# Eight more up products ahead of the dense expert stage, and each row of the second gather used one slot later

## The chip, the cores and the metric

The kernel runs on one core of a Trainium2 chip. The metric is device microseconds (us) of one execution, the median of the runs shown. A profiled execution has a span, from its first to its last instruction, and a time of its own, which is a little longer. Engines are named as in the profile: PE (TensorE), PEld (its weight loads), DVE (VectorE), ACT (ScalarE), POOL (GpSimd) and SP (SyncE, which issues most DMAs).

## The reference

One layer of a hybrid block over 512 tokens of width 1024: a trunk (differential attention beside a gated linear recurrence, merged and projected), and behind it a PEER feed-forward layer with 16384 single-neuron experts. Only the second part matters here. Each token picks 8 x 16 = 128 experts:

```python
q = (hb @ w_q).reshape(PEER_BLOCK, PEER_HEADS, 2, PEER_HALF)
sc = jnp.einsum('thcd,hcnd->thcn', q, sub_keys).astype(jnp.float32)
s1, i1 = lax.top_k(sc[:, :, 0], PEER_TOPK)
s2, i2 = lax.top_k(sc[:, :, 1], PEER_TOPK)
...
top_s, pos = lax.top_k(cand_s, PEER_TOPK)
idx = jnp.take_along_axis(cand_i, pos, axis=-1)
g = jax.nn.softmax(top_s, axis=-1)
u = u_tab[idx]
act = jax.nn.gelu(jnp.einsum('thkd,td->thk', u, hb))
wts = (g * act.astype(jnp.float32)).astype(hb.dtype)
v = v_tab[idx]
return jnp.einsum('thk,thkd->td', wts, v)
```

## The kernel before, in words

The 512 tokens are four blocks of 128. Pass `p0` takes block 0 through the trunk, pass `p1` the other three. The expert layer is then done in two ways.

Blocks 0 and 1 gather. `experts` walks 128 slots; in each, an indirect DMA issued by POOL (L855) brings, for each of the 128 tokens of the block, one row of 2048 numbers (the expert's u and v, 1 MB in all) into one of four buffers `uv`. DVE multiplies the u half with the token and sums (the dot, L862), ACT applies gelu and the weight (L867, L868), and DVE adds the weighted v half to `x1` (L845). The add of a slot is issued behind the dot of the next. A slot's gather is tied to a marked instruction elsewhere in the program (`after(s)`, a dependency given by hand), so that the gathers are spread over the other work. The first gather (block 0) runs beside the trunk of `p1`, the second (block 1, the generator `second`, `table=True`) beside the dense stage.

Blocks 2 and 3 (256 tokens, `NT2`) go through all 16384 experts densely, in 128 chunks of 128 experts. For a chunk, the up product is 8 matmuls of 128x128 by 128x256 over the width and a gelu into a tile `y`; DVE multiplies `y` with the weights that the tokens give to these experts (`o`, L1035); the down product is 4 matmuls of 128x128 by 128x512 that accumulate in `acc` over all chunks. An up product comes in two forms, in `up`: for chunks below `AHEAD` plain, with f32 operands (`u`, and `h2r`, the tokens), and for later chunks split, where `chunk` loads `raw`, ACT rounds it to fp32r (L906), DVE takes the rest (L907), and 24 matmuls form three terms. Split products read the tokens from `p1.h2T`, two tiles of the trunk's pool `ap`.

The order of the dense part:

1. `ups_far`: the first `LEAD` = 26 up products (PSUM tiles `pup`), beside the last top-k work of DVE.
2. `picks_t` transposes the picks (PE `pt`). Then come 16 weight groups (`wbuild`, 16 tokens each): DVE, POOL and ACT build one-hot tiles, PE multiplies them (`pw`, L1010), ACT copies into `wst` (L1011), and SP writes it to a DRAM tensor `w_d` (L1012). An up product (tiles `st`) is given to each group until `AHEAD - 6` are made; the last six are written behind the groups.
3. SP loads the weights back (`w`, L1023), the last two groups' part behind the last write, and the 128 downs follow; from the 24th on, one more (split) up product goes with each down until all are made.

The instructions of an engine run in the order in which a scheduler, working from a simulated timeline, has put them; it may move an up product ahead of where the code has it. `share` counts fractions of a slot (0.2 for each of the far products, 0.5 a weight group, 0.6 a down, 1.1 a down with an up) and starts the next slot of the second gather when a whole one is owed.

## Time and profile before

| | |
|---|---|
| runs | 1903.67 us median of 3 (1903.01 to 1905.06) |
| profiled execution | 1902.58 us, span 1900.8 us |
| PE busy | 1742.3 us (92%) |
| PEld busy | 1371.8 us (72%) |
| DVE busy | 1309.5 us (69%) |
| ACT, POOL busy | 781.8 us (41%), 483.3 us (25%) |
| moved by DMA | 563.37 MB, mean 296 GB/s |
| mean granted clock of PE | 0.949 |

The up products of the dense stage start 933.8 us into the span, the first down at 1193.97. A busy share is a mean over stages with different limits; the rows below are cut by stage for that reason. PE's clock is given as a share of its full 2.4 GHz; 0.5 is its lower level, 1.2 GHz. Matmuls are pipelined; an f32 matmul shows as two records, an fp32r matmul as one.

### The profile page before, as it was taken

The page shows a single profiled execution, that of the slowest core. Times are in us where ns is not written, and L with a number is a line of the kernel's source. Part 1 is how long each engine was busy: PE and PEld are TensorE (multiplying, and loading weights), DVE is VectorE, ACT ScalarE, POOL GpSimd, SP SyncE. Part 2 cuts the span into 40 slices and gives each one's busy share as a digit, 9 for nine tenths or more (in the row PEclk, how much of TensorE's full clock was granted, in tenths as well). Part 3 has the DMA queues.
Part 4 walks back from the last instruction along what each step waited for, and adds up shares of the span by engine and source line. Part 5 has one row for each costly group of instructions (what it writes and reads, how often), then busy time and mean ns, then how long its engine had stood idle before and what let it go on. Part 6 is the DMA issues. An engine that isn't in the chain of part 4 may idle for free.

```text
span 1900.8 us, 25745 instructions
## 1 busy us (share of the span) xinstructions
PE 1742.3 (92%) x9166; PEld 1371.8 (72%) x9166; DVE 1309.5 (69%) x2818; ACT 781.8 (41%) x2193; POOL 483.3 (25%) x375
## 2 busy tenths in 40 slices
PE   7899898889959899979996984899999999999998
PEld 6689797778849677769985884346776677667763
DVE  2241387989999987689999467446676667666662
ACT  3382333767768744254412565012322232222210
POOL 1100001535332233242001365222222232222220
PEclk9899897889969899999998998899999999999999
DMA  7478554887888899987464578999999999999893
GB/s 297 144 272 315 181 186 158 308 291 269 328 287 298 322 400 356 369 310 255 153 220 144 183 274 310 356 373 393 370 367 389 378 365 369 348 350 363 328 354 122
DMA packets 131471, 563.37 MB, mean 296 GB/s; under 512 B 11408, under 2 KB 43280, under 8 KB 88592
## 3 DMA queue, kind: packets, MB, share of 16 engines
q1 hardware_dynamic: 94480, 293.29, 42.6%
q0 software_dynamic: 36864, 268.45, 37.3%
q8 instruction: 72, 1.18, 0.2%
q14 instruction: 55, 0.45, 0.1%
HBM read 539.68 MB, written 22.02 MB: 296 GB/s over the span
## 4 chain that ended last, share of the span: by engine, by line
PE 60%; DVE 14%; issue 9%; DMA 8%; ACT 5%; POOL 3%; DVEq 0%; SPq 0%; POOLq 0%; ACTq 0%
PE acc L210 22%; PE st L210 16%; DMA uv<-in_uv_dram,idx 6%; PE ppq L210 5%; PE pkq L210 5%; POOL uv L855 3%; DVE x1f L845 2%; DVE uv L862 2%; PE pw L1010 1%; PE pvv L210 1%; DMA v<-in_v_t_dram 1%; PE pgt L210 1%; PE psc L511 1%; DVE wl L231 1%; PE pbR L687 1%
## 5 line engine op out<-in xcount | busy, mean ns | idle before, releaser
L855 POOL DMA_INDIRECT uv<-in_uv_dram,idx x256 | 360.0, 1406 | 1067.6 <-DVE x1g L845 265.7
L210 PE MATMUL acc<-v,o 128*128 128x512 f32 x1024 | 449.9, 595 | 20.8 <-DVE o L1035 18.6
L210 PEld LDWEIGHTS acc<-v,o 128*128 128x128 f32 x1024 | 191.8, 191 | 244.9 <-issue 222.4
L210 PE MATMUL st<-a,t 128*128 128x256 f32 x2136 | 282.2, 292 | 0.0
L210 PEld LDWEIGHTS st<-a,t 128*128 128x128 f32 x2136 | 262.5, 191 | 22.5 <-issue 19.6
L845 DVE SCALAR_TENSOR_TENSOR x1g<-uv,e,x1g 128x1024 f32<-128x1024 f32 x128 | 164.1, 1282 | 47.6 <-ACT e L868 47.6
L845 DVE SCALAR_TENSOR_TENSOR x1f<-uv,e,x1f 128x1024 f32<-128x1024 f32 x128 | 163.8, 1280 | 17.2 <-ACT e L877 17.0
L862 DVE SCALAR_TENSOR_TENSOR uv<-uv,h2f 128x1024 f32<-128x1024 f32 x128 | 155.6, 1218 | 28.9 <-DMA uv<-in_uv_dram,idx 28.5
L862 DVE SCALAR_TENSOR_TENSOR uv<-uv,h2g 128x1024 f32<-128x1024 f32 x128 | 155.9, 1218 | 19.6 <-DMA uv<-in_uv_dram,idx 19.6
L867 ACT ACTIVATE e<-e 128x1 f32<-128x1 f32 x128 | 25.9, 202 | 341.4 <-DVE uv L862 341.0
L907 DVE TENSOR_TENSOR t<-raw,t 128x1024 fp32r<-128x1024 f32 x89 | 108.8, 1223 | 74.5 <-ACT t L906 74.5
L1035 DVE TENSOR_TENSOR o<-y,w 128x256 f32<-128x256 f32 x104 | 44.0, 423 | 99.8 <-PE acc L210 99.7
L924 ACT ACTIVATE y<-st 128x256 f32<-128x256 f32 x89 | 34.1, 383 | 179.7 <-PE st L210 177.5
L231 DVE TENSOR_TENSOR wl<-raw,wh 128x1024 fp32r<-128x1024 f32 x76 | 90.9, 1217 | 23.8 <-PE pgt L210 9.5
L906 ACT CAST t<-raw 128x1024 fp32r<-128x1024 f32 x89 | 92.0, 1034 | 25.1 <-PE acc L210 25.1
L210 PE MATMUL pup<-r,u 128*128 128x256 f32 x416 | 90.6, 379 | 1.0 <-DMA u<-in_u_t_dram 1.0
L230 ACT CAST wh<-raw 128x1024 fp32r<-128x1024 f32 x76 | 76.7, 1043 | 28.2 <-PE pwo L714 10.4
L210 PEld LDWEIGHTS pup<-r,u 128*128 128x128 f32 x416 | 78.7, 190 | 12.3 <-issue 1.7
L1010 PE MATMUL pw<-o1s,o 128*128 128x128 f32 x512 | 68.8, 289 | 17.7 <-DVE o L994 13.3
L1009 POOL TENSOR_SCALAR o1s<-iota,r 128x128 f32<-128x128 bf16 x64 | 70.8, 1114 | 41.7 <-issue 14.8
L1010 PEld LDWEIGHTS pw<-o1s,o 128*128 128x128 f32 x512 | 64.5, 199 | 22.8 <-ACT wst L1011 5.7
L210 PE MATMUL pkq<-wh,a 128*128 128x256 f32 x384 | 77.8, 297 | 0.0
(266 smaller groups left out, 3235.5 us busy)
## 6 DMA issues: line engine op xcount, KB each, us to landing
v<-in_v_t_dram SPq DMA_DIRECT2D x64, 1024.0 KB
raw<-in_u_t_dram SPq DMA_DIRECT2D x89, 512.0 KB
u<-in_u_t_dram SPq DMA_DIRECT2D x39, 512.0 KB
w<-in_w_br_dram SPq DMA_DIRECT2D x16, 1024.0 KB
w_d<-wst SPq DMA_DIRECT2D x16, 1024.0 KB
w<-w_d SPq DMA_DIRECT2D x9, 1536.0 KB
w<-in_w_qkv_dram SPq DMA_DIRECT2D x12, 1024.0 KB
raw<-in_w_qkv_dram SPq DMA_DIRECT2D x24, 512.0 KB
```

The source lines that it names most:

```text
L210: nc.tensor.matmul(o, lhs[a], rhs[b], start=start and i == 0, stop=stop and i == len(terms) - 1)
L230: A.copy(hi[:, i : i + 1024], raw)
L231: V.tensor_tensor(lo[:, i : i + 1024], raw, hi[:, i : i + 1024].bitcast(F32), op=ALU.subtract)
L845: V.scalar_tensor_tensor(x1, v_, e_, x1, op0=ALU.mult, op1=ALU.add)
L855: i = nc.gpsimd.indirect_dma_start(out=t, out_offset=None, in_=uv, in_offset=bass.IndirectOffsetOnAxis(ap=idx[:, s : s + 1], axis=0),)
L862: i = V.scalar_tensor_tensor(t[:, 0:D], t[:, 0:D], 1.0, h2, op0=ALU.mult, op1=ALU.mult, accum_out=d)
L906: A.copy(t[:, 0, :], raw)
L907: V.tensor_tensor(t[:, 1, :], raw, t[:, 0, :].bitcast(F32), op=ALU.subtract)
L924: return A.activation(o, S_, AF.Gelu_apprx_tanh)
L1009: e.tensor_scalar(o1, iota, k1, g1, op0=ALU.is_equal, op1=ALU.mult)
L1010: nc.tensor.matmul(pw[:, j, :], o2[:, j, :], o1, start=True, stop=True)
L1035: turn[0] = V.tensor_mul(o.rearrange("p (g t) -> p g t", g=NG), yv, ws[c // WI][:, :, c % WI, :])
```

## The change

It has two parts. In the dense stage `AHEAD` goes from 39 to 47 (`SPARE` = 8 more plain up products, kept in a tile `spare`), `LEAD` from 26 to 31, and the last six (`HELD`) may not be scheduled before the last matmul of the last weight group. Split up products then go with the downs from the 32nd on, so that 81 instead of 89 are split. Their tokens are no longer read from `p1.h2T` but from `h2s`, two tiles that ACT and DVE form from `h2r`; the pool `ap` closes with the trunk to make room, and the trunk's pools stay open until the keys are done. In the second gather (`late`), the dot of a slot, the add of the slot before and the two ACT operations are written behind the issue of the next slot's gather, and the dot may not be scheduled before that slot's marked instruction.

```diff
--- before.py
+++ after.py
@@ -90,9 +90,9 @@
     pp = ctx.enter_context(tc.tile_pool(name="pp", bufs=2))
     dram = ctx.enter_context(tc.tile_pool(name="dram", bufs=1, space=bass.MemoryType.DRAM))
     wp = ctx.enter_context(tc.tile_pool(name="wp", bufs=4))
-    ap = ctx.enter_context(tc.tile_pool(name="ap", bufs=1))
     rg = ctx.enter_context(tc.tile_pool(name="rg", bufs=5))
     trunk = ctx.enter_context(ExitStack())
+    ap = trunk.enter_context(tc.tile_pool(name="ap", bufs=1, side="right"))
     s4 = trunk.enter_context(tc.tile_pool(name="s4", bufs=2, side="right"))
     s2 = trunk.enter_context(tc.tile_pool(name="s2", bufs=5, side="right"))
 
@@ -206,10 +206,13 @@
 
     def mm(o, lhs, rhs, start, stop):
         terms = [(0, 0)] if len(lhs) == 1 or len(rhs) == 1 else [(0, 0), (0, 1), (1, 0)]
-        for i, (a, b) in enumerate(terms):
+        made = [
             nc.tensor.matmul(
                 o, lhs[a], rhs[b], start=start and i == 0, stop=stop and i == len(terms) - 1
             )
+            for i, (a, b) in enumerate(terms)
+        ]
+        return made[0]
 
 
     in_turn = mybir.DependencyInfo(mybir.DependencyClass.Sync, mybir.DependencyReason.SCHED_ONLY)
@@ -849,24 +852,38 @@
             if not table and s < SLOTS:
                 tc.add_manual_dep(i.ins, after(s).ins.name, in_turn, reason="in turn")
 
+        def late(s, t, d, q, w):
+
+            i = V.scalar_tensor_tensor(t[:, 0:D], t[:, 0:D], 1.0, h2, op0=ALU.mult, op1=ALU.mult, accum_out=d)
+            if s + 1 < SLOTS:
+                tc.add_manual_dep(i.ins, mark.ins.name, in_turn, reason="in turn")
+            if before:
+                add(*before.pop(0))
+            A.activation(q, d, AF.Gelu_apprx_tanh)
+            A.activation(w, q, AF.Copy, scale=picks[1][:, s : s + 1])
+            before.append((t[:, D : 2 * D], w))
+
+        waiting = None
         for s in range(SLOTS):
             idx, g = picks
+            mark = after(s)
             t = uvp.tile([P, 2 * D], F32, tag="uv", name=nm("uv"))
             i = nc.gpsimd.indirect_dma_start(
                 out=t, out_offset=None, in_=uv,
                 in_offset=bass.IndirectOffsetOnAxis(ap=idx[:, s : s + 1], axis=0),
             )
-            tc.add_manual_dep(i.ins, after(s).ins.name, in_turn, reason="in turn")
+            tc.add_manual_dep(i.ins, mark.ins.name, in_turn, reason="in turn")
             e = sm.tile([P, 3], F32, tag="e", name=nm("e"))
             d, q, w = e[:, 0:1], e[:, 1:2], e[:, 2:3]
-            i = V.scalar_tensor_tensor(t[:, 0:D], t[:, 0:D], 1.0, h2, op0=ALU.mult, op1=ALU.mult, accum_out=d)
-            behind(i, s + 1)
-            if before:
-                add(*before.pop(0))
             if table:
-                A.activation(q, d, AF.Gelu_apprx_tanh)
-                A.activation(w, q, AF.Copy, scale=g[:, s : s + 1])
+                if waiting:
+                    late(*waiting)
+                waiting = s, t, d, q, w
             else:
+                i = V.scalar_tensor_tensor(t[:, 0:D], t[:, 0:D], 1.0, h2, op0=ALU.mult, op1=ALU.mult, accum_out=d)
+                behind(i, s + 1)
+                if before:
+                    add(*before.pop(0))
 
                 i = A.activation(q, d, AF.Square, scale=GELU_R)
                 behind(i, s + 2)
@@ -875,8 +892,10 @@
                 i = A.activation(w, d, AF.Copy, scale=g[:, s : s + 1])
                 behind(i, s + 2)
                 A.activation(w, q, AF.Identity, scale=w, bias=w)
-            before.append((t[:, D : 2 * D], w))
+                before.append((t[:, D : 2 * D], w))
             yield
+        if waiting:
+            late(*waiting)
         for v_, e_ in before:
             add(v_, e_)
         nc.sync.dma_start(out[t0 : t0 + P, :], x1)
@@ -887,12 +906,13 @@
     NG = NT2 // TG
     NCH = SLOTS
 
-    HEAD, MID = 24, 15
-    AHEAD = HEAD + MID
+
+    HEAD, MID, SPARE = 24, 15, 8
+    AHEAD = HEAD + MID + SPARE
 
     TURN = list(range(HEAD, AHEAD)) + list(range(HEAD)) + list(range(AHEAD, SLOTS))
 
-    LEAD = 26
+    LEAD, HELD = 31, 6
 
     WI = 12
 
@@ -908,17 +928,19 @@
         return t[:, 0, :], t[:, 1, :]
 
 
-    def up(c, S_):
+    def up(c, S_, after=None):
         ks = lambda k: slice(k * P, (k + 1) * P)
         if c < AHEAD:
             u = wp.tile([P, D], F32, tag="raw", name=nm("u"), bufs=3)
             nc.sync.dma_start(u, u_t[c])
             for k in range(KT):
-                mm(S_, [u[:, ks(k)]], [p1.h2r[:, k, :]], k == 0, k == KT - 1)
+                i = mm(S_, [u[:, ks(k)]], [p1.h2r[:, k, :]], k == 0, k == KT - 1)
+                if after is not None and k == 0:
+                    tc.add_manual_dep(i.ins, after.ins.name, in_turn, reason="in turn")
         else:
             uhi, ulo = chunk(u_t, c, "near")
             for k in range(KT):
-                mm(S_, [uhi[:, ks(k)], ulo[:, ks(k)]], [h[:, k, P : 3 * P] for h in p1.h2T], k == 0, k == KT - 1)
+                mm(S_, [uhi[:, ks(k)], ulo[:, ks(k)]], [h[:, k, :] for h in h2s], k == 0, k == KT - 1)
 
     def gelu(o, S_):
         return A.activation(o, S_, AF.Gelu_apprx_tanh)
@@ -951,6 +973,8 @@
 
 
     def kept(c):
+        if HEAD + MID <= c < AHEAD:
+            return spare[:, c - HEAD - MID, :]
         if c >= HEAD:
             return mid.tile([P, NT2], F32, tag="ym", name=nm("y"), bufs=MID)
         if c % WI == 0:
@@ -975,10 +999,10 @@
         pt_ = pool("pt", 2, space=PSUM)
         acc = pa.tile([P, 2, D], F32, tag="acc", name="acc")
 
-        def up_near():
+        def up_near(after=None):
             c = TURN[len(ys)]
             st = pt_.tile([P, 512], F32, tag="st", name=nm("st"))
-            up(c, st[:, 0:NT2])
+            up(c, st[:, 0:NT2], after)
             y = kept(c)
             gelu(y, st[:, 0:NT2])
             ys[c] = y
@@ -1007,9 +1031,10 @@
                     else:
                         e = nc.gpsimd if O1[j] == "P" else V
                         e.tensor_scalar(o1, iota, k1, g1, op0=ALU.is_equal, op1=ALU.mult)
-                    nc.tensor.matmul(pw[:, j, :], o2[:, j, :], o1, start=True, stop=True)
+                    last = nc.tensor.matmul(pw[:, j, :], o2[:, j, :], o1, start=True, stop=True)
                 turn[0] = A.copy(st[:, :, t4 : t4 + 4], pw.rearrange("p t i -> p i t"))
             nc.sync.dma_start(w_d[tg], st)
+            return last
 
         ws, vs = [], []
 
@@ -1040,9 +1065,9 @@
                     mm(acc[:, b, hs], [o[:, bs]], [v_[:, hs]], c == 0, c == NCH - 1)
 
         for tg in range(NG):
-            wbuild(tg)
+            last = wbuild(tg)
             share("w")
-            if len(ys) < AHEAD - 6:
+            if len(ys) < AHEAD - HELD:
                 up_near()
 
             if tg == 7:
@@ -1052,12 +1077,17 @@
                 wload(0, 8, 14)
         wload(0, 14, NG)
         while len(ys) < AHEAD:
-            up_near()
+            up_near(last)
+
+        A.copy(h2s[0], p1.h2r)
+        V.tensor_tensor(h2s[1], p1.h2r, h2s[0].bitcast(F32), op=ALU.subtract)
         for c in range(NCH):
             down(c, ys[c])
-            if c >= HEAD and len(ys) < NCH:
+
+            more = c >= HEAD + SPARE and len(ys) < NCH
+            if more:
                 up_near()
-            share("both" if c >= HEAD and len(ys) < NCH else "down")
+            share("both" if more else "down")
         for b in range(2):
             ob = wp.tile([P, D], F32, tag="raw", name=nm("ob"), bufs=3)
             nc.sync.dma_start(ob, x1_d[1 + b])
@@ -1079,9 +1109,9 @@
     run(p1.rest)
     p1.merge()
     p1.project()
+    run(p1.keys())
     trunk.close()
     mid = ctx.enter_context(tc.tile_pool(name="mid", bufs=1, reuse_waits="tile", side="right"))
-    run(p1.keys())
     when = []
     for name, mark in marks:
         owed[0] += PACE[name]
@@ -1100,6 +1130,9 @@
         yield from experts(P, x1, h2, (p1.idx[:, 0, :], p1.g[:, 0, :]), lambda s: turn[0], True)
 
     ex = second()
+
+    h2s = [mid.tile([P, KT, NT2], F32R, tag=f"h{i}", name=f"h2s{i}") for i in range(2)]
+    spare = mid.tile([P, SPARE, NT2], F32, tag="spare", name="spare")
     ys = ups_far(0, LEAD)
     p1.weights()
     kTs = picks_t()
```

Three places show how the order of the instructions moves. First PE between the last weight group (`pw`) and the first downs (`acc`). Before:

```order
L1010 MATMUL pw_10368<-o1s_10338,o_2093_10369 128x128 x4
L1010 MATMUL pw_10382<-o1s_10338,o_2096_10383 128x128 x4
L210 MATMUL acc<-v_10479,o_10481 128x512 x4
L210 MATMUL acc<-v_10479,o_10487 128x512 x4
L210 MATMUL acc<-v_10500,o_10502 128x512 x4
```

With the change:

```order
L1034 MATMUL pw_10485<-o1s_10441,o_2114_10486 128x128 x4
L210 MATMUL st_10508<-r_6202,u_10509 128x256 x8
L210 MATMUL st_10520<-r_6202,u_10521 128x256 x8
L210 MATMUL st_10532<-r_6202,u_10533 128x256 x8
L210 MATMUL st_10544<-r_6202,u_10545 128x256 x8
L210 MATMUL st_10556<-r_6202,u_10557 128x256 x8
L210 MATMUL acc<-v_10584,o_10586 128x512 x3
L210 MATMUL st_10568<-r_6202,u_10569 128x256 x8
L210 MATMUL acc<-v_10584,o_10586 128x512
L210 MATMUL acc<-v_10584,o_10592 128x512 x4
```

Five whole up products now stand between the two, and a sixth inside the first down. Second, the queue of SP around the last write of the weights (`w_d<-wst`). Before:

```order
L1012 DMA w_d<-wst_10280 128x2048
L1031 DMA v_10479<-in_v_t_dram 128x2x1024
L1031 DMA v_10500<-in_v_t_dram 128x2x1024
L1031 DMA v_10521<-in_v_t_dram 128x2x1024
L1012 DMA w_d<-wst_10339 128x2048
L1023 DMA w_9901<-w_d 128x2x192
L1023 DMA w_10477<-w_d 128x16x192
```

With the change:

```order
L1036 DMA w_d<-wst_10383 128x2048
L1056 DMA v_10584<-in_v_t_dram 128x2x1024
L1056 DMA v_10605<-in_v_t_dram 128x2x1024
L1036 DMA w_d<-wst_10442 128x2048
L1056 DMA v_10626<-in_v_t_dram 128x2x1024
L935 DMA u_10545<-in_u_t_dram 128x1024
L935 DMA u_10557<-in_u_t_dram 128x1024
L1048 DMA w_9980<-w_d 128x2x192
L935 DMA u_10569<-in_u_t_dram 128x1024
L1048 DMA w_10582<-w_d 128x16x192
```

The third load of `v` moves behind the last write, and the loads for the fourth and fifth of the six stand between it and the load of the weights' last part (128x2x192); the sixth one's stands behind that. Third, PE from the last far products (`pup`) through the transposes (`pt`) into the first weight groups. Before:

```order
L210 MATMUL pup_9261<-r_6202,u_9262 128x256 x8
L932 MATMUL pt_1842_9286<-ident,r_6281 128x128 x3
L932 MATMUL pt_1843_9295<-ident,r_6281 128x128 x3
L1010 MATMUL pw_9318<-o1s_9316,o_1847_9319 128x128 x4
L1010 MATMUL pw_9332<-o1s_9316,o_1850_9333 128x128 x4
L210 MATMUL st_9375<-r_6202,u_9376 128x256 x7
L1010 MATMUL pw_9346<-o1s_9316,o_1853_9347 128x128 x4
```

With the change:

```order
L210 MATMUL pup_9328<-r_6202,u_9329 128x256 x8
L954 MATMUL pt_1854_9353<-ident,r_6276 128x128 x3
L954 MATMUL pt_1855_9362<-ident,r_6276 128x128 x3
L210 MATMUL st_9442<-r_6202,u_9443 128x256 x8
L210 MATMUL st_9520<-r_6202,u_9521 128x256 x4
L1034 MATMUL pw_9385<-o1s_9383,o_1859_9386 128x128 x4
L1034 MATMUL pw_9399<-o1s_9383,o_1862_9400 128x128 x4
L210 MATMUL st_9520<-r_6202,u_9521 128x256 x4
L210 MATMUL st_9591<-r_6202,u_9592 128x256 x5
```

Twelve up matmuls now stand ahead of the first weight matmul. Behind them the two kinds alternate, 8 matmuls of `pw` (half a group) and 9 of `st`, eight times (the last with 5); the remaining 192 matmuls of `pw`, twelve groups, stand without up products, where before it was 160, ten groups.

## Rows read from the trace of the kernel before

**Rows 1.** Busy time by stage: PE, PEld, DVE, ACT, POOL, then clock, DMA share, GB/s

```profile
1046.00:1116.00 70.00, 69.57 (x404) 63.89 (x405) 33.63 (x79) 36.70 (x98) 27.38 (x30) 0.96 0.60 209
1116.00:1176.00 60.00, 43.06 (x318) 38.86 (x317) 52.93 (x123) 46.40 (x121) 46.34 (x38) 0.97 0.76 288
1176.00:1194.00 18.00, 0.03 (x1) 0.03 (x1) 2.56 (x5) 0.50 (x2) 1.48 (x1) 0.57 0.80 291
1194.00:1303.00 109.00, 106.84 (x330) 55.03 (x331) 55.56 (x81) 13.98 (x40) 26.78 (x19) 0.98 1.02 385
1303.00:1839.00 536.00, 536.00 (x2703) 371.57 (x2702) 360.12 (x455) 153.53 (x358) 134.74 (x95) 1.00 0.95 364
1839.00:1901.00 62.00, 55.23 (x131) 24.26 (x129) 18.68 (x28) 2.76 (x11) 2.61 (x2) 0.98 0.45 172
```

**Rows 2.** Chain that ended last, pieces of the late stage: start, length, what

```profile
1302.69 6.87 PE acc L210 x16
...
1344.51 5.75 PE st L210 x48
1350.26 6.87 PE acc L210 x16
```

**Rows 3.** The timeline around the first down: PE, then SP's queue

```profile
1173.32 2.02 PE L1010 MATMUL pw<-o1s,o 128*128 128x128 f32 x16 [0.67 <-ACT wst L1011]
1193.97 57.63 PE L210 MATMUL acc<-v,o 128*128 128x512 f32 x128 [18.63 <-DVE o L1035]
1176.36 0.46 SPq L1012 DMA_DIRECT2D w_d<-wst  x1
1190.72 0.88 SPq L1023 DMA_DIRECT2D w<-w_d  x2
```

**Rows 4.** Timeline of PE, end of the far products to the first weight group

```profile
1015.65 10.60 PE L210 MATMUL pup<-r,u 128*128 128x256 f32 x48 [0.95 <-DMA u<-in_u_t_dram]
1044.07 0.90 PE L932 MATMUL pt<-ident,r 128*128 128x128 f32 x3 [5.26 <-DVE r L321]
1046.43 3.78 PE L1010 MATMUL pw<-o1s,o 128*128 128x128 f32 x16 [1.46 <-ACT kTb L937]
```

**Rows 5.** Instructions of the tile pup: count, ns min/median/max, first and last start

```profile
L210 PE MATMUL pup<-r,u x416: 379/379/454, 933.9 to 1025.9; 128*128 128x256 f32 x139
```

**Rows 6.** Timeline of DVE where the second block's picks become ready

```profile
1034.69 1.22 DVE L862 SCALAR_TENSOR_TENSOR uv<-uv,h2g 128x1024 f32<-128x1024 f32 x1
1037.69 1.27 DVE L845 SCALAR_TENSOR_TENSOR x1g<-uv,e,x1g 128x1024 f32<-128x1024 f32 x1
1040.02 2.13 DVE L1009 TENSOR_SCALAR o1s<-iota,r 128x128 f32<-128x128 bf16 x8
1042.79 1.22 DVE L321 TENSOR_REDUCE r<-oh 128x64 f32<-128x1024 bf16 x1
```

**Rows 7.** Timeline of the weight groups: PE with and without ups, one DVE wait

```profile
1106.48 4.05 PE L210 MATMUL st<-r,u 128*128 128x256 f32 x18
1112.15 3.62 PE L210 MATMUL st<-r,u 128*128 128x256 f32 x16
1142.77 1.23 DVE L862 SCALAR_TENSOR_TENSOR uv<-uv,h2g 128x1024 f32<-128x1024 f32 x1 [5.13 <-DMA uv<-in_uv_dram,idx]
1144.75 4.46 PE L1010 MATMUL pw<-o1s,o 128*128 128x128 f32 x24 [5.55 <-DVE o L994]
```

**Rows 8.** Groups of ACT from 1116 to 1176 us: busy us, mean ns | idle before

```profile
L1011 ACT COPY wst<-pw 128x512 f32<-128x512 f32 x40 | 23.1, 578 | 8.1 <-PE pw L1010 8.1
L1006 ACT ACTIVATE o1s<-osq,r 128x128 f32<-128x128 f32 x36 | 16.2, 496 | 0.3 <-DMA w_d<-wst 0.3
L1005 ACT ACTIVATE osq<-iota,r 128x128 f32<-128x128 bf16 x34 | 12.3, 402 | 0.0
```

**Rows 9.** Timeline of the end

```profile
1894.27 2.35 DVE L1064 TENSOR_TENSOR ob<-ob,acc 128x1024 f32<-128x1024 f32 x2 [9.88 <-PE acc L210]
```

**Rows 10.** Waits from 1300 to 1840 us: us in total, times, longest

```profile
POOL uv L855 <- DVE x1g L845: 250.6, 64, 8.9
```

## The prediction

> **What bounds the kernel now.** I read the busy times by stage first. From 1303 to 1839 us PE is busy for all of 536 us at a granted clock of 1.00, its full level, and from 1194 to 1303 for 106.84 of 109 [rows 1]. So from the first down to the end a product is worth its own length, and a wait of DVE, ACT or POOL is not. Ahead of that the same view shows where PE is not full: 43 of 60 us from 1116 to 1176, and nothing in the 18 us before the first down, with the clock at 0.57 at the end of it. The chain of waits gives the late stage's prices: 16 records, two downs, take 6.87 us, so a down 3.433; 48 records, one split product and a second whose down comes later, take 5.75, so a split product 2.875 [rows 2]. The timeline around the first down shows what ended the hole: SP writes the last weights at 1176.36, issues their load at 1190.72, and the first down begins at 1193.97 after 18.63 us of idle PE [rows 3]. A second hole of 18.4 us lies between the end of the far products, 1015.65 + 10.60 = 1026.25, and the first weight matmul at 1046.43; what ends it is DVE, which makes the second block's picks [rows 4].
>
> These prices give the run before back: 1193.97 + 128 downs x 3.433 (439.4) + 89 split products x 2.875 (255.9) = 1889.3. From the first down to 1302.69, where the page's piece begins, 26 downs and 5 split products should take 103.6 us and took 108.7, a loss of 5.1 while PE starts up. With it the sum is 1894.4; the last DVE group, which PE's last down released, begins at 1894.27 [rows 9].
>
> **A, far products.** 26 of them ran from 933.9 [rows 5] to 1026.25 [rows 4], 3.55 us each, stops between them included. Nothing ahead of them moves. 31 end at 933.9 + 31 x 3.55 = 1044.0, so five stand in the hole at no cost. The cover must be there: the picks were ready at 1042.79 + 1.22 = 1044.0 [rows 6]. DVE now makes h2s's second tile ahead of that, twice a 1024-wide f32 pass of 1.22 us (+2.4), and the changed order puts behind it a dot and an add (1.22 + 1.27 [rows 6]) and the eight o1s (2.13). That gives 1041.8. If none of the moves helped it would be 1046.4; that end costs 2.4 us. ACT's cast for h2s is four times a 512-wide copy of 0.578 [rows 8], 2.3 us, in front of gelus that PE does not wait for while its buffers last; I cost it at nothing, at worst 2.3.
>
> **B, four weight groups with products.** From 1044.0: two transposes of 0.9 [rows 4], then 12 up matmuls, 24 records at 3.55/16 = 0.222 (5.3), to 1051.1. Half a group with 9 up matmuls between repeats every 1112.15 - 1106.48 = 5.67 us [rows 7]. Seven such and a last shorter one of 3.9 are 43.6: 1094.7.
>
> **C, twelve groups without.** The ten such groups took from 1112.15 + 3.62 [rows 7] to 1173.32 + 2.02 [rows 3], 59.6 us, 5.96 each. One stop in it was not the groups' own: a dot on DVE waited 5.13 us for its gather and PE 5.55 behind it [rows 7]; without it a group is 5.4. ACT's own three kinds of work come to 51.6 us in it [rows 8], 5.2 a group, so ACT is nearly the bound there, and two groups more cost that too. In `late` a dot stands behind the next slot's mark, so its row has had a slot's time to come, and I expect this stop to go, though a dot can now wait on ACT's copy, which is the mark. I take 5.6, with the ends 5.4 and 5.96: 67.2, and the groups' end T = 1161.9 (1159.5 to 1166.2). It was 1175.3.
>
> **D, the hole before the first down.** It now holds five products; the sixth lies in the first down. The floor stays the path over DRAM, 18.63 us from T, since the write and the load are the same. Three products have their loads at hand: 10.65 us. The fourth and fifth loads can only be issued when the first and second product have freed a buffer, and then stand behind what the queues hold: 18 us x 291 GB/s = 5.2 MB moved in that hole before, with the third v tile (1.05 MB) now in it too. 6.3 MB at 385 GB/s, the best rate of a stage [rows 1], is 16.3 us; no row shows how the queues share, so I let the fourth load land at about 15 and the fifth product end at 22. The ends are 18.6 (the loads slip through) and 25 (they go last). The first down starts at 1161.9 + 22 = 1183.9, 10.1 us earlier than before. The split products' loads, which also stood ahead of the first down before, now come behind; 31 downs cover them.
>
> **E, from the first down to the end.** 439.4 + 81 x 2.875 (232.9) + the sixth product, 3.55 + the loss at the start, 5.1 (none to 5.1, as the hole is now nearly filled) = 681.0, and 1864.9 for the last down. The end after it is unchanged: 1900.8 - 1894.27 = 6.5, a span of 1871.4. The profiled execution before took 1902.58, 1.8 more than its span: 1873.1. Its runs' median stands 1.1 above that time, so **1874**. In parts: 8 split products fewer, -23.0; the first down earlier, -10.1; the sixth product, +3.55.
>
> What `late` itself brings here is little: PE waits for no dot from 1303 to 1839 [rows 1]. It is worth its share of C only. Eight split products fewer also take ACT's roundings and DVE's subtractions away; neither was late, so I count nothing.
>
> **Rivals.** *The transfers take part of it back.* The downs' weights, the split products' loads and the gathers moved 109 x 385 + 536 x 364 = 237 MB by 1839 [rows 1]. Eight loads of 0.52 MB fewer leave 233, and by my sum there are 625.6 us for them, 372 GB/s. The DMA share is already 0.95 there. If 364 were all that the queues give, the stretch would take 640 us, 14 more, and the time be 1888. For it: share 0.95 to 1.02. Against it: 385 GB/s over 109 us, and PE not waiting once in 536 us, so 364 is rather what was asked for. 0.16.
>
> The Trainium skill (DMA: Bandwidth & Descriptors, Specifications) gives a limit of about 358 GB/s from HBM for one core. By that the 233 MB would need 651 us, 25 more, some 1899 (an estimate from that page's figure). Here 385 over 109 us and 364 over 536 stand above it [rows 1], so as a hard limit it does not hold for this core alone; as part of the rival above it gets 0.03 of the chance.
>
> *The gathers run out of buffers (slower).* There are four `uv` buffers, and `late` holds each until the next slot's add. A split product and its down take 6.31 us and owe 1.1 slots: a slot every 5.73 us, four in 22.9. If the buffer came free one slot later, four slots would take 28.7, a slot every 7.16 and so a pair of products 7.88 instead of 6.31. PE would be held through masks that stand behind the waiting dot on DVE: 81 pairs x 1.57 = 127, some 2000 us. For it: POOL already waited 250.6 us, 64 times, for the add that frees a buffer [rows 10]. Against it: in the printed order of DVE a dot stands 2.8 masks behind its mark in this stage, 2.6 before; the add goes with it, so a buffer is held hardly longer. It decides if adds come later against the marks by more than the 8.9 us of the longest wait. 0.03.
>
> That the change does not do what it says can be set aside: the order of PE shows the products where the text says they are.
>
> **How the numbers follow.** Forecast 0.76, the transfers 0.19 with the skill's limit, the buffers 0.03, 0.02 for a stop that I do not see, of which 0.01 ends within 0.2% of before. A measurement of this kernel can tell about 0.2%, 4 us, from no change. Low end: C at 5.4 (-2.4), D at its floor of 18.6 (-3.4), no loss at the start (-5.1) make 1863, and a microsecond for clocks: 1862. High end: C at 5.96 (+4.3), D at 25 (+3), the picks late (+2.4) make 1884; I go on to 1892 to take in the transfers at 364. The forecast's cases and the transfers all end below 1900: faster 0.96, same 0.01, slower 0.03.
>
> **What would show it.** In the timeline of PE: the far products to about 1044 and a weight matmul at about 1051 with no hole of more than 3 us; no up products in the last twelve groups, which end at about 1162; three products at once behind them, a stop of some 4 us, two more, and the first down at about 1184. The w load still about 14 us behind the write. From there no idle PE and 3.433 and 2.875 for a down and a split product. It is wrong if PE shows idle time released by a `v` or `raw` load (the first rival) or by `o` behind a dot (the second), or if the first down stands at 1190 or later, in which case the held loads or the twelve groups were mis-sized, and the timeline tells which.

## The result, and the profile after

| | before | with the change |
|---|---|---|
| median of the runs | 1903.34 us (4, 1900.74 to 1905.06) | 1872.52 us (4, 1867.72 to 1874.02) |
| profiled execution, span | 1900.8 us | 1870.4 us |
| PE busy, mean granted clock | 92%, 0.949 | 93%, 0.956 |

The ratio is 0.9831, with an interval of 0.9811 to 0.9852: faster by 1.7%, 1.5 us under the forecast of 1874. The terms of the sum were less exact than that; some errors were of opposite sign.

Busy time of the changed kernel by stage (stretch, length, then PE, PEld, DVE, ACT, POOL busy with their instructions, PE's clock, DMA share, GB/s), cut at its own events: far products, groups with products, groups without, hole, downs alone, downs with split products, end. It answers to [rows 1].

```profile
934.00:1039.00 105.00, 104.69 (x490) 91.86 (x489) 104.63 (x530) 22.05 (x49) 6.83 (x6) 1.00 0.64 201
1039.00:1088.60 49.60, 49.60 (x296) 45.42 (x295) 29.20 (x68) 28.94 (x83) 24.20 (x22) 1.00 0.64 217
1088.60:1158.60 70.00, 51.21 (x386) 47.06 (x386) 64.88 (x148) 56.42 (x146) 66.25 (x50) 0.98 0.78 285
1158.60:1185.30 26.70, 19.55 (x82) 16.52 (x81) 6.10 (x9) 3.12 (x9) 2.83 (x2) 0.87 1.03 398
1185.30:1298.00 112.70, 108.33 (x258) 49.01 (x256) 49.30 (x75) 9.27 (x33) 24.02 (x18) 0.98 0.98 374
1298.00:1808.00 510.00, 510.00 (x2597) 352.83 (x2596) 344.39 (x437) 147.08 (x342) 136.83 (x90) 1.00 0.95 363
1808.00:1870.00 62.00, 55.80 (x136) 24.83 (x134) 26.73 (x39) 4.25 (x17) 6.97 (x5) 0.97 0.60 226
```

The hole behind the far products is gone, the one before the first down is three quarters full, and PE still never stops once split products go with the downs. In the downs alone PE is idle for 4.4 us, all of it in stops for `v` loads. The kernel before has one such stop there, of 2.16 us:

```profile
1253.76 24.27 PE L210 MATMUL acc<-v,o 128*128 128x512 f32 x56 [2.16 <-DMA v<-in_v_t_dram]
```

PE's timeline of the changed kernel shows where its stops are (start, length, what, records, idle time before it and what ended it); it answers to [rows 3] and [rows 4].

```profile
1009.79 29.52 PE L210 MATMUL pup<-r,u 128*128 128x256 f32 x136
1039.15 0.82 PE L954 MATMUL pt<-ident,r 128*128 128x128 f32 x6
1039.80 5.34 PE L210 MATMUL st<-r,u 128*128 128x256 f32 x24
1044.98 1.95 PE L1034 MATMUL pw<-o1s,o 128*128 128x128 f32 x16
...
1086.47 2.32 PE L210 MATMUL st<-r,u 128*128 128x256 f32 x10
...
1154.95 3.66 PE L1034 MATMUL pw<-o1s,o 128*128 128x128 f32 x30 [3.07 <-POOL o1s L1033]
1158.45 10.53 PE L210 MATMUL st<-r,u 128*128 128x256 f32 x48
1176.13 9.32 PE L210 MATMUL st<-r,u 128*128 128x256 f32 x32 [7.15 <-DMA u<-in_u_t_dram]
1185.29 2.74 PE L210 MATMUL acc<-v,o 128*128 128x512 f32 x6
...
1245.34 41.44 PE L210 MATMUL acc<-v,o 128*128 128x512 f32 x96 [1.50 <-DMA v<-in_v_t_dram]
1289.65 8.80 PE L210 MATMUL acc<-v,o 128*128 128x512 f32 x16 [2.87 <-DMA v<-in_v_t_dram]
```

SP's queue and the chain that ended last show what PE waited for: the fourth held load is issued at 1162.10, behind a write and `v` tiles, and needs 13.89 us; two `v` loads need 21 and 22 us.

```profile
1152.69 6.37 SPq L1056 DMA_DIRECT2D v<-in_v_t_dram  x2
1159.26 0.34 SPq L1036 DMA_DIRECT2D w_d<-wst  x1
1160.99 0.37 SPq L1056 DMA_DIRECT2D v<-in_v_t_dram  x1
1162.10 3.79 SPq L935 DMA_DIRECT2D u<-in_u_t_dram  x2
1172.26 0.38 SPq L1048 DMA_DIRECT2D w<-w_d  x1
```

```profile
1162.10 13.89 DMA u<-in_u_t_dram
...
1224.27 20.93 DMA v<-in_v_t_dram
1245.20 0.14 issue
1245.34 21.81 PE acc L210 x51
1267.15 22.37 DMA v<-in_v_t_dram
```

POOL's wait for the add, which answers to [rows 10], is what it was, and the end [rows 9] starts 6.6 us before the span's end as before:

```profile
POOL uv L871 <- DVE x1g L848: 251.1, 65, 7.6
```

```profile
1863.83 2.35 DVE L1094 TENSOR_TENSOR ob<-ob,acc 128x1024 f32<-128x1024 f32 x2 [9.88 <-PE acc L210]
```

### The profile page after: what moved, and what is told of

It reads as the page before. It is cut to its first block, busy times and chain, and to the rows that moved or that the text cites. A ratio compares the mean times of both kernels' runs of the same rounds, so it can differ in the third digit from the quotient of the medians.

```text
span 1870.4 us, 25606 instructions
## 1 busy us (share of the span) xinstructions
PE 1739.8 (93%) x9102; PEld 1366.9 (73%) x9102; DVE 1303.3 (70%) x2811; ACT 780.0 (42%) x2188; POOL 498.4 (27%) x375
## 4 chain that ended last, share of the span: by engine, by line
PE 73%; DMA 10%; DVE 8%; ACT 4%; issue 4%; POOL 2%; DVEq 0%; SPq 0%; POOLq 0%; ACTq 0%
PE acc L210 22%; PE st L210 15%; PE pup L210 5%; PE ppq L210 5%; DMA uv<-in_uv_dram,idx 5%; PE pgt L210 4%; PE pkq L210 4%; PE pbR L690 4%; PE pbA L683 3%; PE pwo L717 3%; DMA v<-in_v_t_dram 2%; DVE x1f L848 2%; PE pvv L210 2%; PE pw L1034 1%; DVE uv L883 1%
## 5 line engine op out<-in xcount | busy, mean ns | idle before, releaser
L210 PE MATMUL st<-h2s,t 128*128 128x256 f32 x1944 | 252.6, 288 | 0.0
L210 PEld LDWEIGHTS st<-h2s,t 128*128 128x128 f32 x1944 | 235.0, 188 | 20.1 <-issue 17.2
L927 DVE TENSOR_TENSOR t<-raw,t 128x1024 fp32r<-128x1024 f32 x81 | 99.0, 1222 | 69.3 <-ACT t L926 69.3
L210 PE MATMUL pup<-r,u 128*128 128x256 f32 x496 | 107.6, 379 | 0.3 <-DMA u<-in_u_t_dram 0.3
L210 PEld LDWEIGHTS pup<-r,u 128*128 128x128 f32 x496 | 93.9, 190 | 13.4 <-issue 0.8
L926 ACT CAST t<-raw 128x1024 fp32r<-128x1024 f32 x81 | 83.8, 1034 | 23.4 <-PE acc L210 23.4
L1034 PE MATMUL pw<-o1s,o 128*128 128x128 f32 x512 | 66.8, 285 | 18.8 <-ACT wst L1035 8.9
L1033 POOL TENSOR_SCALAR o1s<-iota,r 128x128 f32<-128x128 bf16 x64 | 80.5, 1266 | 10.0 <-issue 4.2
L201 POOL TENSOR_SCALAR sm<-sm 128x1 f32<-128x1 f32 (+4 forms) x24 | 9.6, 398 | 253.6 <-ACT hh L403 111.5
```

The source lines that it names most:

```text
L210: nc.tensor.matmul(o, lhs[a], rhs[b], start=start and i == 0, stop=stop and i == len(terms) - 1)
L926: A.copy(t[:, 0, :], raw)
L927: V.tensor_tensor(t[:, 1, :], raw, t[:, 0, :].bitcast(F32), op=ALU.subtract)
L1033: e.tensor_scalar(o1, iota, k1, g1, op0=ALU.is_equal, op1=ALU.mult)
L1034: last = nc.tensor.matmul(pw[:, j, :], o2[:, j, :], o1, start=True, stop=True)
```

## The experiments

The far products start between 928.3 and 934.3 us in all the profiled executions, of kernels of both sorts (before 933.9, e4 931.0, the change 930.6, e5 932.8). The stage lengths below are therefore taken from an event of the same execution. Runs e1 to e4, e5 to e8, e9 with e10 and e11 with e12 each share a chip and their runs of the kernel before, so their medians can be compared; otherwise the ratios to the kernel before are.

### First group: the two parts, and one piece

**The change again (e1).** 

> The change once more, unaltered, as the yardstick of the runs beside it. If the 3.3 us by which its far products started earlier than in the kernel before (930.63 against 933.93) were only this one execution, they will start between 930 and 934 here, unrelated to the rest; if the change brings them forward, at 930.6 again. Ratio to the kernel before 0.983 to 0.985; the hole between the last weight matmul and the first down is 26 to 27 us again if the held loads' 13.9 us is a property of the order, and nearer 22 if it was an accident of that execution.

Median 1873.29 us, ratio 0.9842 [0.9823, 0.9861]. The far products started at 930.0, the hole was 27.4 us long, the stops for v 2.13 and 1.94 us. Hole and stops belong to the order; the start, with the spread above, does not belong to the change.

**Without the second part (e2).**

```diff
+            i = V.scalar_tensor_tensor(t[:, 0:D], t[:, 0:D], 1.0, h2, op0=ALU.mult, op1=ALU.mult, accum_out=d)
+            behind(i, s + 1)
+            if before:
+                add(*before.pop(0))
             if table:
-                if waiting:
-                    late(*waiting)
-                waiting = s, t, d, q, w
+                A.activation(q, d, AF.Gelu_apprx_tanh)
+                A.activation(w, q, AF.Copy, scale=g[:, s : s + 1])
```

> The change without its second part: the dot of a slot stands again right behind the issue of its own gather, all else as in the change. My theory (the gain is the eight products and the holes, the second part brings little): within 3 us of the change, the twelve groups without products 2 to 4 us longer, since a dot on DVE can wait for its gather in them again, and nothing different behind the first down. Rival (using the rows a slot later is what lets 1.1 slots go by for every pair of products): 10 us or more slower than the change, with PE waiting for o behind a dot.

Median 1878.13 us, ratio 0.9872 [0.985, 0.9894], 4.8 us above the change beside it. The twelve groups took 69.1 us (the change 69.8 and 68.8), so the difference is not there. The same kernel once more:

> The kernel of e2 once more, for a second look at its stops. Theory (they belong to the order): two stops for v at some 60 and 110 us behind the first down again, over 6 us in sum, and 43 us for the 96 records behind the first. Rival (an accident of that execution): 3 to 5 us in sum, as in the change.

Ratio 0.9848 [0.9822, 0.9874], from two runs. The stops in e2 and then in this run (e12):

```profile
1246.75 43.13 PE L210 MATMUL acc<-v,o 128*128 128x512 f32 x96 [4.04 <-DMA v<-in_v_t_dram]
1293.40 8.80 PE L210 MATMUL acc<-v,o 128*128 128x512 f32 x16 [3.52 <-DMA v<-in_v_t_dram]
```

```profile
1038.61 0.52 PE L938 MATMUL pt<-ident,r 128*128 128x128 f32 x3 [1.38 <-DVE r L324]
1041.85 0.87 PE L938 MATMUL pt<-ident,r 128*128 128x128 f32 x3 [2.72 <-DVE r L324]
1042.51 7.39 PE L210 MATMUL st<-r,u 128*128 128x256 f32 x24
...
1249.17 41.44 PE L210 MATMUL acc<-v,o 128*128 128x512 f32 x96 [2.67 <-DMA v<-in_v_t_dram]
1294.18 7.11 PE L210 MATMUL acc<-v,o 128*128 128x512 f32 x16 [3.58 <-DVE uv L865]
```

So the stops were not the same twice: 7.6 us in sum, then 6.3 (expected over 6), and the 43 us behind the first did not come again. The trace names DVE's dot (`uv`) as the end of e12's second stop; the `v` load issued at 1272.00 took 22.0 us and landed at the same time, so the two cannot be told apart there.

What did repeat is in front: PE waits for DVE's picks `r`. Without the second part, five dots and adds of the gather stand ahead of the picks on DVE instead of four (2.5 us a pair), and DVE waits 1.6 us for ACT. The wait and the end of the picks in e12, then the end of the picks in the change:

```profile
1031.53 0.29 DVE L340 TENSOR_REDUCE sm<-r 128x8 f32<-128x128 f32 x1 [1.59 <-ACT r L337]
1040.48 1.22 DVE L324 TENSOR_REDUCE r<-oh 128x64 f32<-128x1024 bf16 x1
```

```profile
1037.57 1.22 DVE L324 TENSOR_REDUCE r<-oh 128x64 f32<-128x1024 bf16 x1
```

Counted from the first far product, the picks are ready at 111.8 us (e2), 113.0 (e12) and 112.9 (e11, below) without the second part and at 108.2 in the change; the first weight matmul comes at 117.5 (e2), 121.1 (e12) and 120.2 (e11), with the second part and the eight products at 113.9 to 115.1 (seven profiles). Not all of this reaches the end. In e12 the first down is 4.5 us later than in the change and the rest takes 0.4 us more; in e2 it is 1.1 us later, and 5.1 us are lost behind it, in the stops and the slower downs behind them. By the ratios the part is worth 1 to 6 us, with intervals that overlap. My theory, which put it into the groups, falls, and so does its rival.

**The second part alone (e3).** The functions `experts` and `late` of the change in the kernel before.

> The kernel before with the second part alone: 39 products ahead as before, the tokens of the split products read from the trunk's tiles as before. My theory: 0 to 6 us faster than the kernel before, all of it in the ten groups without products (59.6 us before, 54 to 58 here); the stretch behind the first down unchanged to 2 us. Rival (it holds buffers longer): slower, with POOL's wait for x1g above 300 us from the first down on (250.6 before). Rival (it carries the gain): faster by over 15 us.

Ratio 1.0007 [0.9993, 1.0021], median 1904.59 us: no difference. The ten groups took 58.6 us instead of 59.6. POOL's wait for x1g from 1300 to 1800 us is 253.3 (before in the same stretch 229.3), and PE never waits for it there. (Earlier, at 1252, the trace puts a stop of PE of 3.6 us down to x1g; a `v` load issued at 1231.45 landed at the same time, after 20.7 us.) Alone, the second part is worth nothing that can be measured. The picks come 109.8 us behind the first far product, in the kernel before 110.1: here the eight o1s still stand ahead of them on DVE, as before.

**The tokens alone (e4; with the wide layout below, e8).** h2s, formed and read as in the change, with `SPARE` 0 and the last six not held.

> The kernel before with one piece of the change: the split products read their tokens from the two compact tiles h2s, not from the trunk's tiles, whose pool closes early; 39 products ahead and the dots as before, the last six products where the kernel before has them. In the trace of the change two split products and two downs came every 12.52 us, in the kernel before every 12.62. Theory (the tiles that the split products read make the difference): 12.52 here too, and 89 x 0.048 = 4.3 us off the time behind the first down; two DVE passes ahead of the picks cost 0 to 2.4 us before it; in sum 2 to 4 us faster than before. Rival (it belongs to the order or to the one execution): 12.62, and 0 to 2.4 us slower than before.

The period was 12.52 us, and the time the same: ratio 1.0001 [0.9986, 1.0016]. The matmuls of the split products, before and here (count, then ns of one, shortest, median, longest):

```profile
L210 PEld LDWEIGHTS st<-a,t x2136: 187/192/192, 1277.4 to 1838.9; 128*128 128x128 f32 x195
L210 PE MATMUL st<-a,t x2136: 278/283/682, 1277.5 to 1839.0; 128*128 128x256 f32 x195
```

```profile
L210 PEld LDWEIGHTS st<-h2s,t x2136: 186/188/190, 1275.0 to 1836.8; 128*128 128x128 f32 x195
L210 PE MATMUL st<-h2s,t x2136: 277/279/683, 1275.0 to 1836.9; 128*128 128x256 f32 x195
```

Each is 4 ns shorter. But the first weight matmul came 116.1 us behind the first far product (before 112.5): ahead of the picks DVE makes h2s, in 2.28 us, and waits 1.6 us for ACT, which takes back 3.6 us. Of the 4.3 us expected behind the first down, 1.2 showed in this execution (699.1 us to the last DVE group, before 700.3). Does the layout in the tile decide?

```diff
+    h2w = [mid.tile([P, KT, 3 * P], F32R, tag=f"h{i}", name=f"h2s{i}") for i in range(2)]
+    h2s = [h[:, :, P : 3 * P] for h in h2w]
```

> The kernel with the tokens alone (e4) with the two token tiles laid out as the trunk's: 384 numbers between one row of tokens and the next, of which the last 256 are read, instead of 256 close together. In e4 two split products and two downs came every 12.52 us, in the kernel before every 12.62. Theory (the layout in the tile decides): 12.62 again. Rival (where the tile lies in the memory, or which pool it is of, decides): 12.52 as in e4. In time nothing over 4 us from either.

12.52 us again, ratio 0.9989 [0.9974, 1.0004]; the last DVE group came 696.6 us behind the first down. It is not the distance between rows. Where the tile lies, or its pool, was not told apart further.

### Second group: the hole

**The v tiles behind the held loads (e5).**

```diff
+                if c in (2, 4):
+                    tc.add_manual_dep(i.ins, loads[-1].ins.name, in_turn, reason="in turn")
```

> The change with two loads moved: the second and third v tile (1 MB each) are loaded behind the load of the sixth held product, where the change has them ahead of the held products' loads. Theory (the fourth held load takes 13.9 us to land because it stands behind v tiles and the last write): it lands in 5 to 8 us, the stop of 7 to 8 us in front of the fourth product shrinks to under 2, the first down comes 18.6 to 21 us behind the last weight matmul instead of 26.7 to 27.4, and the time is 5 to 7 us below the change's (1866 to 1868 beside its 1873). Rival (the v tiles are then late): the first down comes as early, but PE waits 4 us or more for v in the first ten downs, and the time is within 2 us of the change's. Rival (the queues hold it whatever stands in front): the stop stays above 6 us.

`loads` lists the loads of the plain products. The fourth held load landed in 8.2 us instead of 13.9, the hole shrank to 18.8 us and the stop in it to 1.45, but the time is that of the change: 1871.86 us, ratio 0.9832 [0.9815, 0.9849]. It was given back behind the first down:

```profile
1172.62 7.14 PE L210 MATMUL st<-r,u 128*128 128x256 f32 x32 [1.45 <-DMA u<-in_u_t_dram]
1244.83 43.34 PE L210 MATMUL acc<-v,o 128*128 128x512 f32 x96 [6.68 <-DMA v<-in_v_t_dram]
```

From the first down to the last DVE group it takes 683.7 us, the change 678.5 and 678.3. Besides the 6.7 us wait, the 96 records behind it take 43.34 instead of 41.44: the granted clock was 0.93 from 1200 to 1250. PE also waits 2.3 us for the operands of the first split product. My first rival came true, later than it said: with the first down earlier, PE waits for the loads behind it.

**Three held, none held (e6, e7).** `HELD` 3; and `up_near()` instead of `up_near(last)`.

> The change with three products held for the hole before the first down instead of six; the other three go with the weight groups. A group with 2.17 products took 11.55 us in the kernel before (69.3 for six groups), one without takes 5.8 in the change, so a product there costs 2.64: the groups end 7.9 us later, at 1166. Theory (three held products have their loads at hand, only the last three cost the hole): the first down stands 18.6 to 19.2 us behind that, at 1185 as in the change, no product stands in the first down (-3.5), and the time is 3 to 5 us below the change's. Rival (the held products are free where they stand): 3 us or more above the change's.

> The change without the hold: the last six products may be scheduled among the weight groups, as in the kernel before. By the same price of 2.64 us a product the groups end 15.8 us later, at 1174, the first down comes 18.6 to 19.2 behind, at 1193, 8 later than in the change, and the sixth product's 3.5 us in the first down go: 3 to 6 us above the change's time. That is what holding them is worth. Rival (holding is worth nothing, since the hole is then only moved): within 1 us of the change.

Medians 1880.55 us (ratio 0.9865 [0.9845, 0.9885]) and 1883.11 (0.9883 [0.9868, 0.9898]): 9 and 11 us above e5's beside them. So holding three is not as good as holding six, and the theory of e6 falls. Three products moved into the groups delayed the groups' end by 9.0 to 9.5 us (237.0 us behind the first far product, the change and e5 228.0, e1 227.5), 3.0 to 3.2 each, not the 2.64 expected. Six cost 14.9 to 15.4 (242.9), near the 15.8 expected. The hole was 21.3 us with three and 18.6 with none. The 3.5 us that no product in the first down should have given did not come: both stop 4 us for v some 58 us behind the first down, and the 96 records behind take 44. (The trace of e7 is of its slowest execution, 1892.18 us.) By the ratios of either group holding six is worth 8 to 10 us against none, more than expected.

### Third group: the loads behind the first down

**The weights later (e9).**

```diff
+            if j > 2:
+                tc.add_manual_dep(i.ins, turn[0].ins.name, in_turn, reason="in turn")
```

> The change with the loads of the weights' tiles from the fourth on held back until the down before the one at which the code asks for them (12 downs ahead of their first use); in the change two of them (3 MB) are issued together at the 10th down, ahead of six v loads. Theory (the change's stops of 2.1 and 1.9 us for v, at 1245 and 1289, are v loads that stand behind weights nobody needs yet): both stops go or fall under 1.5 us in sum, and the time is 2.5 to 5 us below the change's. Rival (the stretch to the first split product is bound by its bytes, 374 to 390 GB/s all through): a stop of 3 us or more stays there, moved at most, and the time is within 1.5 us of the change's.

Ratio 0.9888 [0.9869, 0.9908], 1882.07 us: slower than the change. Both stops went, but a longer one came at 1328: in SP's order two `raw` loads, which wait for a buffer, now stand ahead of a `v` load, and it is issued when PE needs it. Behind it come slower downs and two stops of 2.3 us each for the split products' `t`, at 1489 and 1571; from the first down to the last DVE group it takes 691.6 us.

```profile
1323.10 4.82 SPq L924 DMA_DIRECT2D raw<-in_u_t_dram  x2
1327.97 0.43 SPq L1058 DMA_DIRECT2D v<-in_v_t_dram  x1
```

```profile
1335.31 9.52 PE L210 MATMUL acc<-v,o 128*128 128x512 f32 x16 [7.20 <-DMA v<-in_v_t_dram]
```

**Both moves of loads (e10).**

> Both moves of loads, that of e5 and that of e9. In e5 the first down came 8.6 us earlier against the last weight matmul than in the change and PE then waited 6.7 us for v at 1245. Theory (the same weights' loads stood ahead of that v): the wait falls under 2 us, the clock stays at 1.00 behind it, and the time is 6 to 10 us below the change's, 1863 to 1867 beside its 1873. Rival (bound by its bytes): the wait stays above 4 us, and the time is within 3 us of e5's 1872.

1858.84 us, ratio 0.9776 [0.9754, 0.9799]: faster than both kernels, 10 to 13 us below the change by the ratios. About half lies in front: against the first far product the first down comes 6.5 us earlier than in the change, though the hole is 22.1 us and not e5's 18.8:

```profile
1167.96 8.82 PE L210 MATMUL st<-r,u 128*128 128x256 f32 x32 [3.10 <-DMA u<-in_u_t_dram]
```

The rest is behind it, 672.1 us to the last DVE group instead of 678.5. From the first down to the end of the split products PE has no idle time:

```profile
1177.00:1283.00 106.00, 106.00 (x257) 48.45 (x255) 51.30 (x78) 9.48 (x35) 26.85 (x18) 1.00 0.99 377
1283.00:1794.00 511.00, 511.00 (x2603) 353.79 (x2602) 343.53 (x436) 146.19 (x341) 135.42 (x90) 1.00 0.97 372
```

The queues are as full there as in the change (0.99 and 0.98), but 106.0 us x 377 = 40.0 MB pass before the first split product instead of 112.7 x 374 = 42.1; the rest, weights not needed yet, goes with the split products, at 372 GB/s instead of 363 and without a stop. So what limited the change there was which bytes stood ahead of which. Why the order of e9, which stops PE at 1328, does not do so here was not traced further. The Trainium skill (DMA: Bandwidth & Descriptors, Queues, rings and completion order) says that a DMA engine takes the descriptors of one queue in the order of its ring; that moving loads behind others in SP's queue removes the stops agrees with it.

**The same without the second part (e11).**

> The kernel of e10 (both moves of loads) without the second part of the change, as e2 is the change without it. In e2 the whole difference from the change, 4.9 us, stood between the first down and the first split product: stops for v of 4.0 and 3.5 us instead of 2.1 and 1.9, and 1.7 us of slower matmuls behind the first. Theory (the second part is worth something only through those stops): e10 has none, so without the second part the time is within 2 us of e10's. Rival (it is worth 5 us wherever PE is bound by what stands behind DVE): 4 to 6 us above e10's, with stops elsewhere.

1866.38 us, ratio 0.9799 [0.978, 0.9819]: 4.4 us above e10 by the ratios, whose intervals overlap at their ends; from the first far product to the last DVE group the traces differ by 4.1. Behind the first down the two are nearly alike (672.9 us here, e10 672.1), without a stop for `v`. The difference begins in front of the weight groups, where PE waits for the picks and restarts slowly:

```profile
1046.71 0.52 PE L940 MATMUL pt<-ident,r 128*128 128x128 f32 x3 [2.72 <-DVE r L324]
1047.07 7.03 PE L210 MATMUL st<-r,u 128*128 128x256 f32 x24
```

The change takes 5.34 us for the same 24 records. The last weight matmul is 5.9 us later than in e10; the hole behind it, 19.5 us instead of 22.1, gives 2.6 back. So here the worth of the second part is in front, not in the `v` stops as this theory had it. Alone (e3) it did not bring the picks forward.

## Why the prediction was right, point by point

- **The bound** held: from the first split product on PE is busy without a gap, and eight split products fewer are worth their length.
- **A.** 31 far products took 108.7 us, 3.51 each instead of 3.55; the start was 3.3 us early by the execution's spread. The picks were ready 108.2 us behind the start, reckoned 107.9, so they were in time. What the prediction got wrong is whose work that is: it gave `late` a share of C only, but `late` is what takes a dot and an add out of DVE's way here, and without it (e2, e11, e12) PE waits.
- **B.** First weight matmul at 1044.98 (1051.1), the products' end at 1088.8: 43.8 us between them (43.6).
- **C** was mis-sized: 69.8 us, 5.82 a group, where I took 5.6. I had laid the 5.55 us stop of [rows 7] to the dot, expecting it to go with `late`; e2 without `late` takes 69.1. In the twelve groups PE waits 8.9 us for ACT's copy `wst`, 5.6 for POOL's `o1s` and 3.5 for DVE's `o`; POOL, which the prediction left out, is busy for 66.25 of the 70 us. The groups end at 1158.6 (1161.9).
- **D** was the term furthest off: 26.7 us against 22, beyond the upper end of 25. The fourth load landed at T + 17.4, not 15, and the two products behind took 9.32 us, not 7.1, at a granted clock of 0.87 in the hole. The mechanism, held loads queued behind what SP issued before, is shown by e5. (The 0.57 that the prediction read as the clock at the end of the hole before is the mean over its 18 us.)
- **E.** 678.5 us to the last DVE group against 681.0. A split product cost 2.83 and not 2.875 (81 x 0.047 = 3.8 us, which e4 shows to come with the tiles h2s), and the loss at the start was 6.5 and not 5.1, with 4.4 of it in stops for `v`. Of the 5.1 us before, which the prediction laid to PE starting up, 2.16 were such a stop too. It also put the first three split loads, now behind the held loads, at nothing: they are 1.6 MB, 4.2 us at 374 GB/s, in the stretch with the stops; no run moved them alone.
- In sum, T came 228.0 us behind the start of the far products, as forecast (A's 1.4 and 1.4 in the first up matmuls offset C's 2.6); the hole was 4.7 us too long, E 2.5 too short, the start 3.3 early. That the time agrees to 1.5 us is partly luck: these errors cancel.
- **Rivals.** By the prediction's own sign, idle time released by a `v` load, its first rival came true in part: 4.4 us, 2.2 more than before, where it was priced at 14. I had priced the transfers over the whole late stage at its mean rate; with the split products PE never waited for them. The buffers did not run out: POOL waited 251.1 us, as in [rows 10].

## What to carry to other kernels

When work is moved into a hole, follow the loads it needs through the queue they are issued on, and the loads that come after it. Here an earlier first down was worth its length only when two groups of loads were put in the order in which PE needs them (e10): each move alone gave nothing or cost time (e5, e9). A part that measures as nothing alone (e3) may be worth some us beside other changes (e11).

## What was not expected of the hardware

- Weight loads and matmuls of the same shape and form took 4 ns more or less, 192 and 283 against 188 and 279 ns, with the tile the tokens are read from (e4, e8); the distance between the rows in the tile made no difference, and whether the tile's place or its pool does is open.
- Stops of 1.5 to 2.7 us for `v` left the next 96 records of downs at 41.44 us (the change, e1, e12); stops of 4.0 to 6.7 us made them 43.1 to 44.1 (e2, e5 to e7). Such a stop costs some 2 us more than its own length.
